# A two-layer hybrid transformer trunk: layer 1's filter spectra, and each norm's sums and first tile, are placed elsewhere

## The chip, the cores and the metric

The kernel runs on one core of one Trainium2 chip. The metric is device time in microseconds (us) of one execution. The core's engines run side by side, each through its own list of instructions in order: TensorE (PE, matrix products; its weight loads stand apart as PEld), VectorE (DVE), ScalarE (ACT), GpSimd (POOL) and SyncE (SP, which issues the transfers). Instructions of different engines wait for one another by semaphores.

## The reference

A trunk of two layers (width 1024) works on 256 latent tokens and 256 context tokens; in the second layer the context only gives keys and values. Cut to what matters here:

```python
for l in range(DEPTH):
    mod = (act_lat @ w_mod[l] + b_mod[l])            # shift, scale and gate for each norm
    sh1, s1, g1, sh2, s2, g2 = split(mod, 6)
    p = modulate(x, norm1_w, sh1, s1) @ w_in         # rms_norm(x, w) * (1 + s) + sh
    x = x + g1 * parallel_mixers(p, attn, lp)        # attention, hyena, pool, gmlp; @ w_out
    h = modulate(x, norm2_w, sh2, s2)
    x = x + g2 * ((silu(h @ wg) * (h @ wu)) @ wd)
return rms_norm(x, final_norm_w)

def hyena_filters(n, lp):                            # inside the hyena mixer
    hdn = ...                                        # small sine network of the positions
    filt = (hdn @ hy_w3) * exp(-t * abs(hy_decay))
    k = concat(fwd, 0, reversed bwd)
    return k / sum(abs(k), axis=0)
kf = rfft(hyena_filters(n, lp), n=2 * n)             # the filter spectra
```

In layer 0 the same is done for the context tokens, so its matrix products carry 512 tokens, those of layer 1 (behind the keys and values) 256. All is float32.

## The kernel before

Activations lie transposed: eight tiles `x[j]` of 128 channels by 512 tokens. A large product is made of three fp32r matmuls (`mm3`, lines 209 to 211): each operand is split into a high part (`whi`, `hh`, a cast on ScalarE, L171 for weights) and a rest (`wlo`, `hl`, a subtraction on VectorE, L174 for weights), and high by high, low by high and high by low are added up in PSUM. Weights come as units of 512 KB in the order of `unit_order`; each of them is one transfer (`load_next`), one cast, one subtraction and 24 matmuls of 128x128 by 512 columns in layer 0. Between the units of layer 0 stand tiles `w_t`, mixed in evenly: a `w_t` tile is a piece of a modulation matrix, and VectorE makes 128 modulation values from it by two reductions (`mod_tile`, L259). Layer 0's FFN has 66 units, in two halves of 22 `w_ff` and 11 `w_dn` units, and 40 such tiles (`TILES1`) are mixed in between the third unit and the last two.

Modulation values that are not made so come in chunks (`CHUNKS`): eight transfers of 256 KB, each with four small matmuls on TensorE (`psmod`, L289) and a transposition on VectorE behind them. `chunk_load` issues the transfers, `chunk_mods` the matmuls. Chunk 4 is loaded in layer 0's product with `w_out`, chunk 5 (layer 1, tiles 16 to 19) in the second half of layer 0's FFN, chunk 6 in layer 1's `w_out`; `LOADAT` holds at which of the eight output tiles.

**A norm.** The last product of a stage ends with `residual` (L1186) for the eighth tile. The squares of the first seven tiles have been added into `acc` on VectorE by then (`sumsq_add`), the eighth's are made by ScalarE (`last_sq`, L326). `rstd` adds both over the channels with one-column matmuls (`pmss`, L336), four pairs for 512 tokens and two pairs for 256; VectorE scales the sums (L340), GpSimd takes the power -1/2 (L342), VectorE writes it on a diagonal (`dg`, L350), and TensorE spreads it over the partitions (`psrb`, L357, a float32 matmul). `norm_tiles` then makes the eight tiles of the product's input: VectorE multiplies with `psrb` (`nt`, L372), ScalarE scales and shifts each half of the tokens (`nh`, L375) and casts (`hh`, L376), VectorE subtracts (`hl`, L381). The products behind it begin with tile 0: `k_major` (tile `pmk`) with the first three `w_ff` units in norm 2, `wide_gen` (tile `pmw`, L621) in norm 1 of layer 1. The last norm has the sums and GpSimd's step alone; its transposed tiles (`psfin`) are scaled and stored.

**The spectra of layer 1** are made in the second half of layer 0's FFN by `spectra_gen(1)`, a generator that goes one step behind each output tile: transfers of `w3` and `dec`, four float32 matmuls with the network's output (`pspf`, L454), the window and the sums of absolute values, a reciprocal (L475), splits, and five spectra (A0, A1, B0, B1, C0) of six fp32r matmuls each (`pssp`) against constants.

The program is written unit by unit; a scheduler orders each engine's instructions from it, so those of neighbouring steps lie between one another.

## Time and profile before

| what | value |
|---|---|
| median of 3 runs | 1348.98 us (1348.16 to 1349.43) |
| the profiled execution | 1349.05 us |
| its span | 1347.3 us |
| PE busy | 1304.3 us (97%) |
| VectorE busy | 925.6 us (69%) |
| ScalarE busy | 607.1 us (45%) |
| GpSimd busy | 64.2 us (5%) |
| mean granted TensorE clock | 0.981 |

The span is what the profile's times count from; 1.75 us of the execution lie outside of it. A busy PE is one in which a matmul is in flight. The granted clock is 1.00 where TensorE ran at 2.4 GHz and 0.50 where it ran at 1.2 GHz; a stretch between holds some of both.

### The profile page before, as it was taken

Reading aid. Unit: us, or ns where it says so; the run is one execution under the profiler, and the core shown is the slowest. Engines: PE = TensorE matmul, PEld = TensorE weight load, DVE = VectorE, ACT = ScalarE, POOL = GpSimd, SP = SyncE. Lnnn points to the kernel's source line nnn. Section 1 sums busy time; section 2 is a strip of 40 time slices with the busy share of each in tenths; the row PEclk is TensorE's granted clock in tenths of the full one; section 3 lists DMA queues with packets and bytes.
Section 4 is the critical chain, followed back from the end, with each engine's and each line's share of the span. In section 5 each row is a group of like instructions: output and inputs, shape, how many; then the busy total and the mean of one; then the engine's idle time right before and its main releaser. Section 6 shows DMA issues by size and latency. Waiting matters only on the chain.

```text
span 1347.3 us, 20114 instructions
## 1 busy us (share of the span) xinstructions
PE 1304.3 (97%) x7778; PEld 1135.4 (84%) x7778; DVE 925.6 (69%) x1578; ACT 607.1 (45%) x1059; POOL 64.2 (5%) x69
## 2 busy tenths in 40 slices
PE   4999999999999999999999999989999999999997
PEld 4778788888888877888888887879989998999997
DVE  3688778798977456666566666856789866655554
ACT  3563323467753326222222224255458854543443
POOL 0001400300000000000000000001310000000000
PEclk7999999999999999999999999989999999999999
DMA  9541334343345452555455553433334467465561
GB/s 345 199 140 62 102 111 145 114 141 106 121 142 166 162 188 68 166 162 167 144 175 167 160 165 124 160 126 124 127 116 144 138 194 254 143 187 179 182 187 49
DMA packets 68640, 203.86 MB, mean 151 GB/s; under 512 B 7616, under 2 KB 13888, under 8 KB 68544
## 3 DMA queue, kind: packets, MB, share of 16 engines
q1 hardware_dynamic: 68544, 202.58, 46.7%
q8 instruction: 61, 1.00, 0.3%
q14 instruction: 35, 0.29, 0.1%
HBM read 201.50 MB, written 1.05 MB: 150 GB/s over the span
## 4 chain that ended last, share of the span: by engine, by line
PE 72%; issue 16%; DVE 6%; ACT 2%; POOL 1%; DMA 1%; SPq 0%; DVEq 0%; POOLq 0%; ACTq 0%
PE pmn L209 14%; PE pmn L211 14%; PE pmn L210 14%; PE pmd L210 3%; PE pmd L211 3%; PE pmd L209 3%; PE pmb L209 2%; PE pmb L211 2%; PE pmb L210 2%; DVE wlo L174 2%; PE pmw L621 2%; PE psav L1132 1%; PE pmw L623 1%; PE pmw L622 1%; PE pspt L1110 1%
## 5 line engine op out<-in xcount | busy, mean ns | idle before, releaser
L171 ACT CAST whi<-raw 128x1024 fp32r<-128x1024 f32 (+2 forms) x312 | 288.1, 929 | 493.3 <-PE pmn L210 208.4
L209 PE MATMUL pmn<-hh,whi 128*128 128x512 f32 (+1 forms) x1328 | 450.8, 339 | 0.3 <-DVE vst L665 0.3
L211 PE MATMUL pmn<-hh,wlo 128*128 128x512 f32 (+1 forms) x1328 | 448.8, 338 | 0.3 <-DVE wlo L174 0.3
L210 PE MATMUL pmn<-hl,whi 128*128 128x512 f32 (+1 forms) x1328 | 449.0, 338 | 0.0
L174 DVE TENSOR_TENSOR wlo<-raw,whi 128x1024 fp32r<-128x1024 f32 (+2 forms) x312 | 335.9, 1079 | 164.4 <-ACT whi L171 161.4
L209 PEld LDWEIGHTS pmn<-hh,whi 128*128 128x128 f32 x1328 | 252.8, 190 | 27.3 <-DVE vst L665 0.7
L211 PEld LDWEIGHTS pmn<-hh,wlo 128*128 128x128 f32 x1328 | 252.5, 190 | 27.5 <-issue 1.1
L210 PEld LDWEIGHTS pmn<-hl,whi 128*128 128x128 f32 x1328 | 252.6, 190 | 26.2 <-issue 0.5
L259 DVE CUSTOM_DVE_ANT_0 junk<-raw,cb,pack_a 128x1024 bf16<-128x1024 f32 x136 | 176.8, 1300 | 1.5
L209 PE MATMUL pmd<-hh,whi 128*128 128x512 f32 (+1 forms) x352 | 120.2, 341 | 0.0
L210 PE MATMUL pmd<-hl,whi 128*128 128x512 f32 (+1 forms) x352 | 119.3, 339 | 0.0
L211 PE MATMUL pmd<-hh,wlo 128*128 128x512 f32 (+1 forms) x352 | 118.5, 337 | 0.0
L210 PEld LDWEIGHTS pmd<-hl,whi 128*128 128x128 f32 x352 | 66.9, 190 | 7.9 <-issue 1.2
L209 PEld LDWEIGHTS pmd<-hh,whi 128*128 128x128 f32 x352 | 66.9, 190 | 7.4 <-issue 0.7
L211 PEld LDWEIGHTS pmd<-hh,wlo 128*128 128x128 f32 x352 | 66.9, 190 | 7.3 <-issue 0.5
L1242 DVE TENSOR_TENSOR sg<-sg,pmn 128x512 f32<-128x512 f32 (+1 forms) x42 | 23.3, 554 | 67.5 <-PE pmn L211 67.5
L342 POOL TENSOR_TENSOR rs<-rs,halfexp 128x4 f32<-128x4 f32 (+1 forms) x5 | 5.4, 1078 | 971.6 <-DVE rs L340 971.6
L621 PE MATMUL pmw<-whi,hh 128*128 128x512 f32 (+1 forms) x112 | 45.1, 403 | 6.8 <-ACT hh L376 6.8
L375 ACT ACTIVATE nh<-nt,mod,amod 128x256 f32<-128x256 f32 x56 | 30.7, 593 | 42.4 <-DVE nt L372 37.1
L622 PE MATMUL pmw<-wlo,hh 128*128 128x512 f32 (+1 forms) x112 | 43.5, 388 | 0.0
L623 PE MATMUL pmw<-whi,hl 128*128 128x512 f32 (+1 forms) x112 | 43.2, 389 | 0.0
L1186 DVE SCALAR_TENSOR_TENSOR x<-pmd,mod,x 128x256 f32<-128x256 f32 x48 | 21.8, 477 | 24.8 <-PE pmd L211 24.8
(270 smaller groups left out, 1888.6 us busy)
## 6 DMA issues: line engine op xcount, KB each, us to landing
raw<-in_w_ff SPq DMA_DIRECT2D x88, 512.0 KB, 3.7
raw<-in_w_nar SPq DMA_DIRECT2D x84, 512.0 KB, 3.7
raw<-in_w_t SPq DMA_DIRECT2D x68, 512.0 KB, 3.7
raw<-in_w_dn SPq DMA_DIRECT2D x44, 512.0 KB, 4.1
raw<-in_w_mod SPq DMA_DIRECT2D x56, 256.0 KB, 5.7
raw<-in_w_wide SPq DMA_DIRECT2D x16, 512.0 KB, 3.7
raw<-in_w_out SPq DMA_DIRECT2D x16, 512.0 KB, 4.3
raw<-in_w_br SPq DMA_DIRECT2D x48, 128.0 KB, 2.1
```

The source lines that it names most:

```text
L171: S.copy(hi[:, :n], raw[:, :n])
L174: V.tensor_sub(lo[:, :n], raw[:, :n], f32(hi[:, :n]))
L209: T.matmul(o, lhsT=wh, rhs=xh, start=first, stop=False)
L210: T.matmul(o, lhsT=wh, rhs=xl, start=False, stop=False)
L211: T.matmul(o, lhsT=wl, rhs=xh, start=False, stop=last)
L259: r = V.tensor_tensor_reduce(out=junk, in0=raw, in1=cb[:, s, :], scale=1.0, scalar=bmod[:, l, i : i + 1], op0=ALU.mult, op1=ALU.add, accum ...
L375: S.activation(h[:, a0:a1], t[:, a0:a1], AF.Identity, bias=sh, scale=a[:, j, k : k + 1])
L621: T.matmul(os_[t][:, :n], lhsT=hh[:, sl], rhs=wh, start=(kt == 0), stop=False)
L622: T.matmul(os_[t][:, :n], lhsT=hh[:, sl], rhs=wl, start=False, stop=False)
L623: T.matmul(os_[t][:, :n], lhsT=hl[:, sl], rhs=wh, start=False, stop=(kt == 7))
L1186: V.scalar_tensor_tensor(x[j][:, sl], o[:, sl], mod[l][:, gi * 8 + j, k : k + 1], x[j][:, sl], op0=ALU.mult, op1=ALU.add)
L1242: V.tensor_mul(sg[:, CS], sg[:, CS], o[:, CS])
```

## The change

1. **Tiles in place of a chunk.** Chunk (1, 4) is dropped; its tiles (1, 16) to (1, 19) become `w_t` tiles, 44 in place of 40 in layer 0's FFN, mixed in between its sixth unit and its last four.
2. **Sums in two calls.** `rstd` is split: `sums_of` for `acc` is issued ahead of the last residual, and one for the last squares behind it.
3. **First tile.** For norms without a `between` argument (norm 2 of both layers, norm 1 of layer 1) `norm_tiles` makes tile 0 by two `scalar_tensor_tensor` on VectorE (x times scale times `psrb`, one for each 256 tokens), from which ScalarE writes `hh` and VectorE `nh`.
4. **Filters.** The transfers of `w3` and `dec` for layer 1 go to layer 0's `w_out`, ahead of chunk 4's. The four `pspf` matmuls are written at layer 0's second norm, and their results are copied to SBUF by ScalarE (`filter_keep`).
5. **Spectra.** `spectra_gen(1)` ends with the split parts, which get the tiles `hh4` to `hh7` and `hl4` to `hl7`. The matmuls of the five spectra are written from the last residual of layer 0's FFN on, around `rstd` and `rstd_bcast`; VectorE's part of A0, A1 and C0 (`spectrum_out`) goes between the norm's tiles 2 to 4.
6. The transfer of `skip` is issued behind those of the transform's constants.

```diff
-LOADAT = (4, 6)
+LOADAT = 4
-TILES1 = [(1, i) for i in (*range(16), *range(20, 24), *range(24, 40), *range(44, 48))]
+TILES1 = [(1, i) for i in (*range(40), *range(44, 48))]
-CHUNKS += [(l, tuple(range(4 * c, 4 * c + 4))) for l, c in ((0, 10), (1, 4), (1, 10))]
+CHUNKS += [(l, tuple(range(4 * c, 4 * c + 4))) for l, c in ((0, 10), (1, 10))]
...
-            ff = ff[:3] + mix(ff[3:-2], TILES1) + ff[-2:]
+            ff = ff[:6] + mix(ff[6:-4], TILES1) + ff[-4:]
...
+    def sums_of(o, v, c0, c1, first, last):
         nt = (c1 - c0) // P
-        o = bank("ss")
         for t in range(nt):
             sl = slice(c0 + t * P, c0 + t * P + P)
-            for i, v in enumerate(sums):
-                T.matmul(
-                    o[:, t : t + 1], lhsT=v[:, sl], rhs=ones[:, 0:1], start=(i == 0), stop=(i == len(sums) - 1)
-                )
+            T.matmul(
+                o[:, t : t + 1], lhsT=v[:, sl], rhs=ones[:, 0:1],
+                start=first and t == 0, stop=last and t == nt - 1,
+            )
...
+                short = between is None and j == js[0]
+                if not short:
+                    V.tensor_mul(t[:, sl], x[j][:, sl], rb[:, sl])
                 for a0, a1, k in spans:
                     sh = mod[l][:, 24 * which + j, k : k + 1]
-                    S.activation(h[:, a0:a1], t[:, a0:a1], AF.Identity, bias=sh, scale=a[:, j, k : k + 1])
-                S.copy(hi[:, sl], h[:, sl])
+                    if short:
+                        V.scalar_tensor_tensor(
+                            t[:, a0:a1], x[j][:, a0:a1], a[:, j, k : k + 1], rb[:, a0:a1], op0=ALU.mult, op1=ALU.mult
+                        )
+                        S.activation(hi[:, a0:a1], t[:, a0:a1], AF.Identity, bias=sh)
+                        V.tensor_scalar(h[:, a0:a1], t[:, a0:a1], sh, None, op0=ALU.add)
...
+    def filter_mm(l, p, o):
+        w3, _, f = flt[l]
+        f[p, o] = side("pf")
+        T.matmul(f[p, o], lhsT=hk[:, p * P : p * P + P], rhs=w3[o], start=True, stop=True)
+
+    def filter_keep(l, p, o):
+        f = flt[l][2]
+        t = t2(s="fo")
+        S.copy(t, f[p, o])
+        f[p, o] = t
...
+            if j == KT - 1:
+                so = bank("ss")
+                sums_of(so, acc, C0, NTOK, True, False)
+                if full:
+                    filter_mm(1, 0, 0)
             residual(o, j, 2)
...
-            if j == LOADAT[0]:
-                chunk_load(4 if full else 6)
-        last = last_sq(x, C0, NTOK)
-        r2 = rstd([acc, last], C0, NTOK)
+            if j == LOADAT:
+                if full:
+                    filters_load(1)
+                chunk_load(4 if full else 5)
+        sums_of(so, last_sq(x, C0, NTOK), C0, NTOK, False, True)
+        r2 = rstd(so, C0, NTOK)
+        if full:
+            filter_mm(1, 0, 1)
         chunk_mods(BUB[0])
         rb = rstd_bcast(r2, C0, NTOK)
+        if full:
+            filter_mm(1, 1, 0)
         chunk_mods(BUB[1])
...
+        if full:
+            for po in ((0, 0), (0, 1), (1, 0)):
+                filter_keep(1, *po)
+            filter_mm(1, 1, 1)
+            filter_keep(1, 1, 1)
...
-        last = last_sq(x, C0, NTOK)
-        r2 = rstd([acc, last], C0, NTOK)
+        sums_of(so, last_sq(x, C0, NTOK), C0, NTOK, False, True)
+        r2 = rstd(so, C0, NTOK)
         if full:
-            chunk_mods(BUB[0])
+            spectrum_out(1, "B0", skip)
+            spectrum_mm(1, "B1", parts, fwd, nyq)
+            spectrum_out(1, "B1", skip)
+            spectrum_mm(1, "A0", parts, fwd, nyq)
             rb = rstd_bcast(r2, C0, NTOK)
-            chunk_mods(BUB[1])
+            spectrum_mm(1, "A1", parts, fwd, nyq)
+            spectrum_mm(1, "C0", parts, fwd, nyq)
```

What the scheduler makes of it is seen in the lists of instructions. First TensorE's at layer 0's second norm, from the small matmuls of the chunk (`psmod`) to the matmul that spreads the norm's factor (`psrb`); in the list before one sum of `acc` and five transfers' `psmod` stand ahead of these rows.

```order
L289 MATMUL psmod_4684<-raw_4558,csf 32x128 x4
L289 MATMUL psmod_4684<-raw_4560,csf 32x128
L336 MATMUL pmss_4671<-ones,sq_4669 128x1
L336 MATMUL pmss_4671<-ones,acc_4369 128x1
L336 MATMUL pmss_4671<-ones,sq_4669 128x1
L336 MATMUL pmss_4671<-ones,acc_4369 128x1
L336 MATMUL pmss_4671<-ones,sq_4669 128x1
L336 MATMUL pmss_4671<-ones,acc_4369 128x1
L336 MATMUL pmss_4671<-ones,sq_4669 128x1
L289 MATMUL psmod_4684<-raw_4560,csf 32x128 x3
L289 MATMUL psmod_4684<-raw_4562,csf 32x128 x4
L357 MATMUL psrb_4703<-dg_4701,ones 128x512
```

The same place now, from the last matmul of `w_out` (`pmn`) on.

```order
L211 MATMUL pmn_4644<-mgh_4349,wlo_4598 128x512
L334 MATMUL pmss_4675<-ones,acc_4369 128x1 x4
L463 MATMUL pspf_4680<-w_1060_4548,hyh 128x512
L463 MATMUL pspf_4694<-w_1061_4549,hyh 128x512
L334 MATMUL pmss_4675<-ones,sq_4684 128x1 x4
L289 MATMUL psmod_4696<-raw_4556,csf 32x128 x4
L289 MATMUL psmod_4696<-raw_4558,csf 32x128 x4
L289 MATMUL psmod_4696<-raw_4560,csf 32x128 x4
L289 MATMUL psmod_4696<-raw_4562,csf 32x128 x4
L289 MATMUL psmod_4696<-raw_4564,csf 32x128
L360 MATMUL psrb_4715<-dg_4713,ones 128x512
L289 MATMUL psmod_4696<-raw_4564,csf 32x128 x3
```

Four sums stand ahead of the residual's wait and four behind it; between them stand two filter matmuls (`pspf`; the `w` that they read is `w3`). Behind `psrb` come the rest of the chunk's fifth transfer and its last three, 15 small matmuls. Of the other two filter matmuls one lies among `k_major`'s rows and one behind them.

Second, TensorE's list at layer 1's first norm, before, with the end of dropped chunk (1, 4).

```order
L289 MATMUL psmod_7371<-raw_7300,csf 32x128 x4
L289 MATMUL psmod_7371<-raw_7302,csf 32x128 x4
L336 MATMUL pmss_7358<-ones,sq_7356 128x1
L336 MATMUL pmss_7358<-ones,acc_4887 128x1
L336 MATMUL pmss_7358<-ones,sq_7356 128x1
L336 MATMUL pmss_7358<-ones,acc_4887 128x1
L336 MATMUL pmss_7358<-ones,sq_7356 128x1
L336 MATMUL pmss_7358<-ones,acc_4887 128x1
L336 MATMUL pmss_7358<-ones,sq_7356 128x1
L289 MATMUL psmod_7371<-raw_7304,csf 32x128 x4
L289 MATMUL psmod_7371<-raw_7306,csf 32x128 x4
L357 MATMUL psrb_7390<-dg_7388,ones 128x512
```

The same place now; `pssp_7341` is B1, `pssp_7350` A0 and `pssp_7361` A1.

```order
L210 MATMUL pssp_7341<-fl_7164,dft_fh_869 128x512
L211 MATMUL pssp_7341<-fh_7163,dft_fl_870 128x512
L209 MATMUL pssp_7350<-fh_7099,dft_fh_863 128x512
L334 MATMUL pmss_7315<-ones,sq_7329 128x1 x4
L210 MATMUL pssp_7350<-fl_7100,dft_fh_863 128x512
L211 MATMUL pssp_7350<-fh_7099,dft_fl_864 128x512
L209 MATMUL pssp_7350<-fh_7104,dft_fh_869 128x512
L210 MATMUL pssp_7350<-fl_7105,dft_fh_869 128x512
L211 MATMUL pssp_7350<-fh_7104,dft_fl_870 128x512
L360 MATMUL psrb_7359<-dg_7357,ones 128x512
L209 MATMUL pssp_7361<-fh_7099,dft_fh_863 128x512
L210 MATMUL pssp_7361<-fl_7100,dft_fh_863 128x512
```

Eight spectrum matmuls lie between the two groups of sums (the last three are seen here), five ahead of `psrb`, and twelve (A1 and C0) between `psrb` and the first `pmw`; four of B0's and one of B1's stay among the `pmd` matmuls of the FFN's second half.

Third, ScalarE's list at the same norm, before, from the last squares to the second tile's cast.

```order
L326 ACTIVATE sq_7356<-x_4367 128x512
L375 ACTIVATE nh_7397<-nt_7396,mod_89,amod_92 128x256 x2
L375 ACTIVATE nh_7405<-nt_7404,mod_89,amod_92 128x256
L376 CAST hh_7398<-nh_7397 128x512
L375 ACTIVATE nh_7405<-nt_7404,mod_89,amod_92 128x256
L375 ACTIVATE nh_7434<-nt_7433,mod_89,amod_92 128x256
L376 CAST hh_7406<-nh_7405 128x512
```

The same now.

```order
L326 ACTIVATE sq_7329<-x_4367 128x512
L556 COPY spec_7339<-pssp_7320 128x512
L556 COPY spec_7348<-pssp_7341 128x512
L384 ACTIVATE hh_7377<-nt_7375,mod_89 128x256 x2
L387 ACTIVATE nh_7386<-nt_7385,mod_89,amod_92 128x256 x2
L389 CAST hh_7387<-nh_7386 128x512
```

Two copies of spectra (B0, B1) stand ahead of the first tile, whose cast and whose interleaved scaling of tile 1 are gone.

## Rows read from the trace of the kernel before

**Rows 1.** The page's first part: engine, busy us (share of span), instructions.
```profile
PE 1304.3 (97%) x7778; PEld 1135.4 (84%) x7778; DVE 925.6 (69%) x1578; ACT 607.1 (45%) x1059; POOL 64.2 (5%) x69
```

**Rows 2.** Windows: busy us (instructions) of PE, PEld, DVE, ACT, POOL, clock, DMA, GB/s.
```profile
502.00:508.00 6.00, 2.62 (x3) 1.00 (x4) 2.87 (x5) 2.69 (x6) 0.00 (x0) 0.50 0.23 82
...
888.00:896.00 8.00, 5.04 (x12) 3.14 (x13) 4.76 (x9) 5.24 (x11) 0.00 (x0) 0.50 0.00 0
...
1146.00:1150.00 4.00, 4.00 (x23) 4.00 (x22) 3.43 (x12) 3.94 (x11) 0.00 (x0) 0.58 0.02 7
```

**Rows 3.** Timeline, layer 0's second norm: start, us, engine, instruction, [idle before <-releaser].
```profile
496.07 1.72 PE L289 MATMUL psmod<-raw,csf 128*32 128x128 f32 x50
...
497.71 0.38 PE L336 MATMUL pmss<-ones,sq 128*128 128x1 f32 x2
...
499.48 0.16 DVE L340 TENSOR_SCALAR rs<-pmss 128x4 f32<-128x4 f32 x1
499.56 1.28 DVE L259 CUSTOM_DVE_ANT_0 junk<-raw,cb,pack_a 128x1024 bf16<-128x1024 f32 x1
499.72 1.98 POOL L342 TENSOR_TENSOR rs<-rs,halfexp 128x4 f32<-128x4 f32 x1 [232.71 <-DVE rs L340]
...
502.48 2.08 PE L357 MATMUL psrb<-dg,ones 128*128 128x512 f32 x2 [2.47 <-DVE dg L350]
...
507.45 1.65 PE L209 MATMUL pmk<-hh,whi 128*128 128x512 f32 x3 [2.90 <-ACT hh L376]
...
511.83 0.40 PE L209 MATMUL pmk<-hh,whi 128*128 128x512 f32 x1
```

**Rows 4.** The page's groups: one half tile on ScalarE, one on VectorE.
```profile
L375 ACT ACTIVATE nh<-nt,mod,amod 128x256 f32<-128x256 f32 x56 | 30.7, 593 | 42.4 <-DVE nt L372 37.1
...
L1186 DVE SCALAR_TENSOR_TENSOR x<-pmd,mod,x 128x256 f32<-128x256 f32 x48 | 21.8, 477 | 24.8 <-PE pmd L211 24.8
```

**Rows 5.** Timeline of PE alone, second half of layer 0's FFN.
```profile
821.07 1.13 PE L454 MATMUL pspf<-w,hyh 128*128 128x512 f32 x2 [0.31 <-DMA w<-in_hy_w]
...
823.25 1.13 PE L454 MATMUL pspf<-w,hyh 128*128 128x512 f32 x2 [0.37 <-DMA w<-in_hy_w]
...
826.76 1.88 PE L454 MATMUL pspf<-w,hyh 128*128 128x512 f32 x4
828.07 0.79 PE L209 MATMUL pmd<-hh,whi 128*128 128x512 f32 x1
828.70 0.40 PE L210 MATMUL pmd<-hl,whi 128*128 128x512 f32 x1
```

**Rows 6.** Windows of layer 0's FFN, columns as in group 2.
```profile
514.00:690.00 176.00, 176.00 (x778) 145.85 (x777) 111.64 (x155) 50.69 (x63) 0.00 (x0) 1.00 0.49 153
...
830.00:850.00 20.00, 20.00 (x86) 15.76 (x85) 18.56 (x31) 6.80 (x10) 0.00 (x0) 1.00 0.31 102
850.00:866.00 16.00, 16.00 (x71) 12.98 (x71) 15.02 (x22) 5.35 (x7) 0.00 (x0) 1.00 0.57 174
```

**Rows 7.** Timeline, layer 1's first norm.
```profile
886.08 1.01 POOL L342 TENSOR_TENSOR rs<-rs,halfexp 128x4 f32<-128x4 f32 x1 [384.39 <-DVE rs L340]
...
887.87 2.08 PE L357 MATMUL psrb<-dg,ones 128*128 128x512 f32 x2 [1.49 <-DVE dg L350]
...
892.91 0.58 PE L621 MATMUL pmw<-whi,hh 128*128 128x256 f32 x1 [2.96 <-ACT hh L376]
...
897.87 0.40 PE L621 MATMUL pmw<-whi,hh 128*128 128x512 f32 x1
```

**Rows 8.** Timeline, layer 1's second norm: the first tile.
```profile
1143.43 1.08 DVE L372 TENSOR_TENSOR nt<-x,psrb 128x256 f32<-128x256 f32 x3 [0.85 <-PE psrb L357]
...
1145.32 0.62 PE L209 MATMUL pmk<-hh,whi 128*128 128x256 f32 x3 [1.93 <-ACT hh L376]
```

**Rows 9.** Timeline, the last norm: three sums, then their scaling.
```profile
1339.45 0.38 PE L336 MATMUL pmss<-ones,sq 128*128 128x1 f32 x2 [0.69 <-ACT sq L326]
...
1340.31 0.16 DVE L340 TENSOR_SCALAR rs<-pmss 128x2 f32<-128x2 f32 x1 [1.37 <-PE pmss L336]
```

More of the change, by code (lines that the diff above doesn't have):

```diff
@@ L436, in trunk_kernel, with filters_load @@
     spectra = {}
-    def spectra_gen(l):
-        if l == 0:
-            yield from mlp_gen()
+    flt = {}
+    def filters_load(l):
         w3 = [t2(s="w3") for _ in range(2)]
@@ L446, in spectra_gen @@
             SY.dma_start(out=dec[o], in_=I["hy_decay"][l, o * 512 : o * 512 + 512].partition_broadcast(P))
+        flt[l] = w3, dec, {}
+    def filter_mm(l, p, o):
[7 more added lines that the diff above has]
+        f[p, o] = t
+    def spectra_gen(l):
+        if l == 0:
+            yield from mlp_gen()
+            filters_load(l)
+        _, dec, fs = flt[l]
+        for o in range(2):
             S.activation(dec[o], dec[o], AF.Abs)
@@ L449, in spectra_gen @@
         for p in range(2):
-            f = [t2(s="fo") for _ in range(2)]
+            f = []
             s_, d_ = t2(s="fs"), t2(s="fd")
             for o in range(2):
-                pf = side("pf")
-                T.matmul(pf, lhsT=hk[:, p * P : p * P + P], rhs=w3[o], start=True, stop=True)
+                if l == 0:
+                    filter_mm(l, p, o)
+                    f.append(t2(s="fo"))
+                else:
+                    f.append(fs[p, o])
                 win = t2(s="win")
                 S.activation(win, dec[o], AF.Exp, scale=hy_negt[:, p : p + 1])
-                V.tensor_mul(f[o], pf, win)
+                V.tensor_mul(f[o], fs[p, o], win)
                 if p == 0:
@@ new lines, in spectra_gen @@
+                if l == 0:
+                    hi, lo = t2(F32R, "fh"), t2(F32R, "fl")
+                else:
+                    n = 4 + 2 * k + p
+                    hi = xp.tile([P, NTOK], F32R, tag=f"hh{n}", name=nm("fh"))
+                    lo = xp.tile([P, NTOK], F32R, tag=f"hl{n}", name=nm("fl"))
+                split(hi, lo, sd[p][k])
+                ps_.append((hi, lo))
+            parts.append(ps_)
+            if l == 0:
+                if k == 0:
+                    yield
+                for name in (("A0", "A1"), ("B0", "B1", "C0"))[k]:
+                    spectrum_mm(l, name, parts, fwd, nyq)
+                    spectrum_out(l, name, skip)
+            else:
+                yield
@@ new lines, in spectra_gen, with spectrum_mm, spectrum_out @@
+        flt[l] = parts, fwd, nyq, skip
+    def spectrum_mm(l, name, parts, fwd, nyq):
+        k, col, mat = {
+            "A0": (0, 0, fwd), "A1": (0, 128, fwd), "B0": (1, 0, nyq), "B1": (1, 384, fwd), "C0": (0, 128, nyq)
+        }[name]
+        o = side("sp")
+        for p in range(2):
+            h, lo = mat[p]
+            mm3(o, h[:, col : col + P], lo[:, col : col + P], *parts[k][p], p == 0, p == 1)
+        spectra.setdefault(l, {})[name] = o
+    def spectrum_out(l, name, skip):
+        t = t2(s="spec")
+        o = spectra[l][name]
+        if name in ("A0", "A1", "C0"):
+            V.tensor_add(t, o, skip)
+        else:
+            S.copy(t, o)
+        spectra[l][name] = t
@@ L649, in trunk_kernel @@
         else:
-            for h in norm_tiles(l, 0, x, rb, 0, NTOK, range(KT)):
+            for i, h in enumerate(norm_tiles(l, 0, x, rb, 0, NTOK, range(KT))):
                 hs.append(h)
                 os_ = next(w0)
-                chunk_mods(REST)
+                if i in (2, 3, 4):
+                    spectrum_out(1, ("A0", "A1", "C0")[i - 2], flt[1][3])
         sg_ = spectra_gen(0) if l == 0 else iter(())
@@ L1260, in trunk_kernel @@
                         done()
+                if half == 1 and j == KT - 1:
+                    for _ in sg_:
+                        pass
+                    so = bank("ss")
+                    sums_of(so, acc, C0, NTOK, True, False)
+                    if full:
+                        parts, fwd, nyq, skip = flt[1]
+                        spectrum_mm(1, "B0", parts, fwd, nyq)
                 residual(o, j, 5)
@@ L1269, in trunk_kernel @@
                 next(sg_, None)
-                if full and half == 1 and j == LOADAT[1]:
-                    chunk_load(5)
-            for _ in sg_:
-                pass
-        last = last_sq(x, C0, NTOK)
-        r2 = rstd([acc, last], C0, NTOK)
+        sums_of(so, last_sq(x, C0, NTOK), C0, NTOK, False, True)
+        r2 = rstd(so, C0, NTOK)
         if full:
-            chunk_mods(BUB[0])
+            spectrum_out(1, "B0", skip)
+            spectrum_mm(1, "B1", parts, fwd, nyq)
+            spectrum_out(1, "B1", skip)
+            spectrum_mm(1, "A0", parts, fwd, nyq)
             rb = rstd_bcast(r2, C0, NTOK)
-            chunk_mods(BUB[1])
+            spectrum_mm(1, "A1", parts, fwd, nyq)
+            spectrum_mm(1, "C0", parts, fwd, nyq)
     final_weigh(KT - 1)
```

38 lines of the change are left out of this document (13 added, 25 removed).

## The prediction, on record before the changed kernel ran

> **What bounds the kernel now.** The page's busy times come first: TensorE is busy for 1304.3 us of the span of 1347.3, VectorE for 925.6, ScalarE for 607.1 [rows 1]. So time can be won in two ways: work taken off TensorE where it is dense, and shorter waits in the few gaps. The windows by stage come next. In layer 0's FFN TensorE is busy without a break (176.00 of 176.00 us, 20.00 of 20.00, 16.00 of 16.00 [rows 6]); what leaves it there shortens the span one for one. In the second of these, VectorE is busy for 18.56 of 20 us, so a second engine is near its limit. The gaps are the norms. There the clock is the second price: 0.50 from 502 to 508 and from 888 to 896, 0.58 from 1146 to 1150 [rows 2]; 0.50 is 1.2 GHz, so matmuls behind the gap take twice as long. The timeline shows the chain of a gap: last sums, VectorE's scaling, GpSimd's power, `psrb`, the first tile, the first `pmk` or `pmw` [rows 3, 7].
>
> **Terms from rows.** A 512-column fp32r matmul at full clock takes 16.00 / 71 = 0.225 us [rows 6]. Two filter matmuls and one `pmd` lie between 826.76 and 828.70: (1.94 - 0.225) / 2 = 0.86 us for one filter matmul [rows 5]. `psrb` has the same shape and type: 2.08 us as the gaps show it [rows 3, 7], about 1.0 at full clock (0.86 and the pipeline's end). Seven sums end just before 499.48: (499.43 - 497.71) / 7 = 0.25 each [rows 3]. A `psmod` record takes 1.72 / 50 = 0.034 [rows 3].
>
> **Dense part of layer 0's FFN.** 25 of 30 spectrum matmuls leave it: 25 x 0.225 = 5.6 us. Two of the four filter matmuls go into the norm's gap: 2 x 0.86 = 1.7; the other two stay in dense stretches, at the norm's product. The waits for `w3` (0.31 and 0.37) go [rows 5], since the transfers are now issued some three output units, about 16 us, ahead of use: 0.7. Together **8.0 us**. VectorE gets eight more L259 of 1.28 us, 10.2 us, less a little work on the dropped chunk; ScalarE four copies of half a microsecond. I cost them at nothing: TensorE covers them, as VectorE has 64 us free of 176 in the longest stretch [rows 6]. Without this cover they cost what the third and fourth cases say. The dropped chunk's 2 MB are replaced by four tiles of 512 KB, so transfers stay equal.
>
> **Gap at layer 0's second norm.** The last residual's product ends near 495.9. Four sums (1.0), two filter matmuls (1.7) and four sums (1.0) in one queue end at about 499.5: the scaling at 499.48 stays where it is. The earlier sums gain nothing here, because the filters take their place. GpSimd's power took 1.98 us with an L259 of a tile alongside it on VectorE [rows 3] and 1.01 in the other gap, where none ran [rows 7]; the tile leaves this gap: gain 0.97 (bounds 0 and 0.97; I take the near row, since it is the same operation). From `psrb`'s end (502.48 + 2.08 = 504.56) to the first `pmk` at 507.45 it was 2.89 us [rows 3]. Now one half tile on VectorE, 0.48, then two on ScalarE, 2 x 0.59 [rows 4], with hand-offs 1.73: gain 1.16. The rest is the clock. Before, TensorE idled for 2.47 and then 2.90 us, and its clock came back only at 511.83; the ten matmuls between 507.45 and there took 4.38 us, where 2.25 would do: a loss of 2.1 [rows 3]. Now `psrb` is wanted at 501.5, after an idle of 0.9, and 30 `psmod` records (1.0) fill the wait for the first tile. If the clock stays up, `psrb` gives 1.1 and the matmuls 2.1 more: 0.97 + 1.16 + 1.1 + 2.1 = 5.3. If it falls, the leftover `psmod` take 2.0 at half speed and hold the first `pmk` until 502.48 - 0.97 + 2.08 + 2.0 = 505.6: a gain of 1.85. No row decides between these; I take the middle, **3.6**.
>
> **Gap at layer 1's first norm.** Eight spectrum matmuls (1.8) and the first four sums (1.0) hold the last four sums until about 886.05, some 0.2 later than the 885.84 that GpSimd's start at 886.08 implies [rows 7]. `psrb` comes at 888.1. TensorE is idle for only some 0.9 us ahead of it instead of 1.49, and the twelve matmuls of A1 and C0 stand behind it, so I take the clock to stay up: `psrb` ends at 889.1, A1 and C0 at 889.1 + 12 x 0.225 = 891.8. The first tile is ready at 889.1 + 1.73 = 890.8, hidden. Before, `pmw` began at 892.91 at half clock and had done 12 matmuls of 256 and 6 of 512 columns by 897.87 [rows 7]; at full clock these are worth 12 x 0.225 = 2.7, a start at 895.2. Gain 895.2 - 891.8 = **3.4**. If the clock falls all the same, `psrb` ends at 890.2 and the twelve take 4.96 us, as those of before did: 895.1, a gain of 0 if the clock is back by then and a loss of 2.2 if the next products are slow too. Bounds -2.2 and 3.4. The two copies on ScalarE run while it waits.
>
> **The clock rule.** The Trainium skill (TensorE: Matmul & The Clock Gate, HAM oscillation) says that a TensorE that waits between groups of matmuls drops to half rate, and that each next group then starts slow. Both gaps keep waits after the change, so by this rule alone the second case below holds, at 1338.0; the rows agree as to both gaps before.
>
> **The other norms.** Layer 1's second norm: first tile from 1143.43 to 1145.32, 1.89 us [rows 8]; now 0.48 + 0.59 and hand-offs, 1.2: gain 0.7. One sum fewer stands behind the last squares, here and in the last norm, where three sums and the hand-off took 0.86 us [rows 9]: about 0.22 each. Together **1.1** (bounds 0.4, if transfers hold the small matmuls there, and 2.8, if the slow stretch from 1146 to 1150, worth (1 - 0.58) x 4 = 1.7, goes as well [rows 2]).
>
> **Sum.** 8.0 + 3.6 + 3.4 + 1.1 = 16.1. The profiled execution took 1349.05 us, 1.75 outside the span, and stands 0.07 above the median: 1349.05 - 16.1 = 1332.9.
>
> **The cases.**
> First, as summed: **1332.9**, its own range 1329.3 (5.3 and 2.8 instead of 3.6 and 1.1) to 1337. Chance 0.60.
> Second, the clock falls in both gaps all the same. For it: it fell in both before, and a queue of one-column sums stands in each. Against it: shorter idle times. 8.0 + 1.85 + 0 + 1.1 = 11.0: **1338.0**, down to a gain of 8.7, 1340.3, with the loss of 2.2. Chance 0.20.
> Third, VectorE becomes the bound where layer 1's filters are made. From 830 to 866 it is busy for 33.6 of 36 us [rows 6]; 44 tiles over 56 units in place of 40 over 61 add 0.13 tile, 0.35 us, to a unit of 24 x 0.225 = 5.4 us: 2.3 more, 35.9 of 36. It decides if the work comes in bunches; a late `wlo` then costs up to 3 us: **1336**. Chance 0.12.
> Fourth, on the slow side: TensorE waits for `wlo` throughout layer 0's FFN, because a tile's two reductions (2.6) stand ahead of it. A unit with a tile, a `wlo` and the gating's work fills nearly 5.4 us. The point is 16.1 / 56 = 0.29 us of waiting for each of the 56 units; at 0.4 it loses 22.4: **1355**. Against it: VectorE was busy for only 112 of 176 us, and units are split ahead of use [rows 6]. Chance 0.05, of which 0.02 within 0.2%.
> Fifth, the change does not do what it says: the filters wait for `w3` in the gap, with the sums queued behind. At 2 us each it costs 4: **1337**. Against it is the lead of 16 us. Chance 0.03.
>
> **How the numbers follow.** Two runs' medians can be told apart from 0.2%, 2.7 us. Faster: all cases but the fourth, 0.95; same 0.02; slower 0.03. The range takes the first case's low end and the second's high end: 1329 to 1341; the fourth and the far ends are left out.
>
> **What would show it.** Right: no `pspf` and about five `pssp` in the FFN's second half; GpSimd's power near 1.0 in layer 0's second norm; `psrb` near 1.0 and a clock near 1.00 behind layer 1's first norm, with `pmw` right behind the spectra; first tiles 0.7 to 1.2 us shorter. Wrong: windows with 0.50 behind `psrb`; PE waits for `wlo` in layer 0's FFN; waits for `w` ahead of the sums. The forecast falls if the dense part doesn't lose its 8 us.

## The result and the profile after

The changed kernel takes 1328.99 us (median of 4 runs, 1327.81 to 1329.54); the kernel before took 1349.2 beside it (1348.16 to 1349.55). The ratio is 0.9852, with an interval of 0.984 to 0.9864. Run again later beside other kernels, it took 1327.89 against 1346.67: 0.986 (0.9839 to 0.9881). By the medians the change is worth 20.2 us in the first comparison and 18.8 in the second. The forecast was 1332.9, from 1329 to 1341; the result lies on the low end of this range (0.01 us below it; the later median lies 1.1 below it, with the kernel before 2.5 faster as well).

The first part of the page of the changed kernel, to be read against [rows 1]:

```profile
PE 1292.9 (98%) x7714; PEld 1128.2 (85%) x7714; DVE 935.6 (71%) x1599; ACT 608.6 (46%) x1060; POOL 61.9 (5%) x69
```

TensorE is busy for 11.4 us less, while the span is shorter by 21.3 (1347.3 to 1326.0). Little computation has gone: filters and spectra are all still made, and only the dropped chunk's 64 `psmod` records, some 2.2 us at 0.034 each, are gone. The rest of the fall in busy time is matmuls that ran at half clock and now run at full clock; the remaining 9.9 us of the gain are idle time.

Windows of the changed kernel behind the three norms (columns as in [rows 2]), and one of the end of layer 0's FFN:

```profile
500.00:504.00 4.00, 3.49 (x40) 2.34 (x40) 3.69 (x8) 2.54 (x6) 0.00 (x0) 1.00 0.02 6
...
872.00:876.00 4.00, 4.00 (x18) 3.02 (x19) 2.92 (x7) 1.80 (x4) 0.00 (x0) 1.00 0.00 0
...
1126.00:1130.00 4.00, 4.00 (x25) 4.00 (x25) 3.38 (x11) 3.82 (x10) 0.00 (x0) 0.68 0.02 9
...
830.00:850.00 20.00, 20.00 (x87) 16.02 (x86) 20.00 (x33) 9.04 (x13) 0.00 (x0) 1.00 0.38 132
```

The clock is 1.00 where [rows 2] had 0.50 twice; in layer 1's second norm it is 0.68 here, and was 1.00 in the second profile of the same kernel. From 830 to 850 VectorE is busy for 20.00 of 20 us; the kernel before had 19.69 in its fullest such stretch (840 to 860), so this is not far from what it was.

Layer 0's second norm now (timeline; start, us, engine, instruction, idle before it), against [rows 3]:

```profile
494.33 1.96 PE L463 MATMUL pspf<-w,hyh 128*128 128x512 f32 x4
...
496.13 0.95 PE L334 MATMUL pmss<-ones,sq 128*128 128x1 f32 x8
...
497.12 0.16 DVE L343 TENSOR_SCALAR rs<-pmss 128x4 f32<-128x4 f32 x1 [1.27 <-PE pmss L334]
497.36 1.01 POOL L345 TENSOR_TENSOR rs<-rs,halfexp 128x4 f32<-128x4 f32 x1 [232.66 <-DVE rs L343]
...
499.15 1.13 PE L360 MATMUL psrb<-dg,ones 128*128 128x512 f32 x2 [0.86 <-DVE dg L353]
500.20 1.07 PE L289 MATMUL psmod<-raw,csf 128*32 128x128 f32 x30
...
501.78 0.96 PE L209 MATMUL pmk<-hh,whi 128*128 128x512 f32 x3 [0.51 <-ACT hh L384]
```

Idle times of 0.86 and 0.51 us stand where 2.47 and 2.90 stood. `psrb` takes 1.13 in place of 2.08, and the 30 leftover `psmod` records fill most of the wait for the first tile.

Layer 1's first norm, against [rows 7]:

```profile
870.12 1.01 POOL L345 TENSOR_TENSOR rs<-rs,halfexp 128x4 f32<-128x4 f32 x1 [371.75 <-DVE rs L343]
...
871.91 1.13 PE L360 MATMUL psrb<-dg,ones 128*128 128x512 f32 x2 [0.80 <-DVE dg L353]
...
875.40 0.39 PE L211 MATMUL pssp<-fh,dl 128*128 128x512 f32 x1
...
875.63 0.28 PE L676 MATMUL pmw<-whi,hh 128*128 128x256 f32 x1
```

`pmw` follows the last spectrum matmul without a wait.

**Stage by stage.** The last squares (L326, ScalarE) of layer 0's second norm and of layer 1's first one cut each profile into three stretches:

| profile | start to squares, layer 0 | to squares, layer 1 | to the end | span |
|---|---|---|---|---|
| before | 496.97 | 386.43 | 463.90 | 1347.3 |
| changed | 494.69 | 372.62 | 458.69 | 1326.0 |
| changed, second profile | 496.00 | 372.77 | 457.33 | 1326.1 |

Ahead of the first squares the two kernels issue nearly the same work, yet 2.28 us are won there. The windows of the wait in the inverse transform, of before and of after, show where most of it is:

```profile
160.00:170.00 10.00, 8.30 (x30) 6.23 (x29) 8.60 (x18) 3.17 (x6) 1.51 (x2) 0.85 0.32 110
```

```profile
160.00:170.00 10.00, 8.30 (x36) 6.33 (x35) 7.98 (x16) 3.70 (x7) 0.84 (x2) 1.00 0.28 88
```

The first product behind the wait, of before and of after:

```profile
166.14 0.49 PE L209 MATMUL psiv<-yh,dft_ih 128*128 128x512 f32 x1 [1.47 <-ACT yh L142]
```

```profile
165.38 0.49 PE L209 MATMUL psiv<-yh,dft_ih 128*128 128x512 f32 x1 [1.47 <-ACT yh L142]
```

TensorE is busy for 8.30 us in both, with a wait of 1.47 us in both, and the clock fell behind it in one only. From these rows to the squares it is 330.83 us before and 329.31 after: 1.5 of the 2.28. Over ten profiles, of the changed kernel and of those below whose TensorE does the same up to there, the first stretch is 494.69 to 497.92 us; the kernel before's 496.97 lies inside. So this part of the difference is chance: it comes and goes from run to run.

### The profile page after: what moved, and what is told of

The parts are those of the page before. It is cut to its first block, busy times and chain, and to the rows that moved or that the text cites. A ratio compares the mean times of both kernels' runs of the same rounds, so it can differ in the third digit from the quotient of the medians.

```text
span 1326.0 us, 19996 instructions
## 1 busy us (share of the span) xinstructions
PE 1292.9 (98%) x7714; PEld 1128.2 (85%) x7714; DVE 935.6 (71%) x1599; ACT 608.6 (46%) x1060; POOL 61.9 (5%) x69
## 4 chain that ended last, share of the span: by engine, by line
PE 75%; issue 16%; DVE 5%; ACT 2%; POOL 1%; DMA 0%; DVEq 0%; POOLq 0%; ACTq 0%
PE pmn L209 14%; PE pmn L211 14%; PE pmn L210 14%; PE pmd L209 3%; PE pmd L210 3%; PE pmd L211 3%; PE pmb L209 2%; PE pmb L210 2%; PE pmb L211 2%; PE pmw L676 2%; PE pmw L678 2%; PE pmw L677 2%; PE psav L1188 1%; PE pspt L1166 1%; DVE wlo L174 1%
## 5 line engine op out<-in xcount | busy, mean ns | idle before, releaser
L259 DVE CUSTOM_DVE_ANT_0 junk<-raw,cb,pack_a 128x1024 bf16<-128x1024 f32 x144 | 187.0, 1299 | 1.4
L387 ACT ACTIVATE nh<-nt,mod,amod 128x256 f32<-128x256 f32 x51 | 28.0, 594 | 24.4 <-DVE nt L377 19.2
```

The source lines that it names most:

```text
L259: r = V.tensor_tensor_reduce(out=junk, in0=raw, in1=cb[:, s, :], scale=1.0, scalar=bmod[:, l, i : i + 1], op0=ALU.mult, op1=ALU.add, accum ...
L387: S.activation(h[:, a0:a1], t[:, a0:a1], AF.Identity, bias=sh, scale=a[:, j, k : k + 1])
```

## The experiments

Changes of stretches below are against the changed kernel's second profile; changes of medians against its 1327.89.

**The changed kernel again.**

> The changed kernel itself once more, beside the next three on one chip, so that they can be compared directly. Theory A (the part of its gain that lies ahead of the first edit, 2.3 us of clock in the first 494 us of the profile, is chance): ratio to the kernel before nearer to 0.9865 than to 0.985, and in another profile the stretch ahead of layer 0's second norm may be as long as before. Theory B (that part belongs to the change): ratio 0.985, the stretch 2 us shorter again.

Its first stretch was 496.00 us in place of 494.69, and in layer 1's second norm the clock stayed at 1.00. At 165 us it held as in the first profile; most of the 1.3 us lies ahead of that, in the first product of layer 0, where the clock was 0.90 from 30 to 60 in place of 0.95. The ratio of 0.986 is nearer to A, but the intervals of both runs hold both values; the ten first stretches decide for A.

**The clock by itself.** The kernel before, with matmuls that compute nothing needed:

```diff
+    def warmup(v, n, c0=0, c1=512):
+        for _ in range(n):
+            T.matmul(side("fill")[:, : c1 - c0], lhsT=ones, rhs=v[:, c0:c1], start=True, stop=True)
...
         chunk_mods(BUB[0])
+        if full:
+            warmup(acc, 2)
         rb = rstd_bcast(r2, C0, NTOK)
         chunk_mods(BUB[1])
+        if full:
+            warmup(acc, 2)
```

and in the same way one and two of them at layer 1's first norm.

> The kernel before with nothing but needless matmuls added (float32, 128x512, 0.86 us each at full clock, results unused): in layer 0's second norm one among the last sums, one ahead of psrb and two behind it, in layer 1's first norm one among the last sums and two behind psrb. It measures the clock by itself. Theory A (the clock falls there because TensorE waits, and that costs psrb 1.1 and the first products 2.1 to 2.2 in each of the two gaps): about 4 to 6.5 us faster than before, 1342.5 to 1345, clock near 1.00 behind both psrb, one added matmul ahead of the sums costing some tenths. Theory B (the clock falls because of the one-column sums, whatever is beside them): no gain, or up to 2 us slower: 1349 to 1351.

1342.57 us against 1346.34 beside it, ratio 0.9966 (0.9955 to 0.9977): 3.8 us faster by the medians, 4.6 by the ratio. Windows of the two gaps, against the first two of [rows 2]:

```profile
502.00:508.00 6.00, 4.11 (x11) 2.11 (x12) 3.82 (x6) 3.41 (x7) 0.00 (x0) 1.00 0.26 87
888.00:896.00 8.00, 7.04 (x42) 6.26 (x43) 6.47 (x12) 8.00 (x17) 0.00 (x0) 1.00 0.00 0
```

Work that only keeps TensorE busy brings the clock to 1.00 in both. In the profile the second stretch is 3.3 us shorter than before's and the third 3.2: together A's upper figure of 6.5. Of the third's 3.2 only 2.7 lie ahead of layer 1's second norm, and the rest, where nothing was added, is not the edit's. The runs as a whole give less, 3.8 to 4.6.

**Spectra back in the FFN.**

```diff
-            if l == 0:
+            if True:
...
-            spectrum_out(1, "B0", skip)
-            spectrum_mm(1, "B1", parts, fwd, nyq)
-            spectrum_out(1, "B1", skip)
-            spectrum_mm(1, "A0", parts, fwd, nyq)
             rb = rstd_bcast(r2, C0, NTOK)
-            spectrum_mm(1, "A1", parts, fwd, nyq)
-            spectrum_mm(1, "C0", parts, fwd, nyq)
```

> The changed kernel with one part undone: all 30 spectrum matmuls of layer 1 stand in the second half of layer 0's FFN again; the gap at layer 1's first norm is left to the norm alone (chunk (1, 4) stays dropped). Both theories: 25 x 0.225 = 5.6 us more in the dense part. Theory A (clock stays up without them): the first pmw starts 1.73 us behind the end of psrb in place of 2.7, and the sums lose 0.2 of delay: 5.6 - 1.2 = 4.4 slower than the changed kernel, 1333.4, ratio 0.988. Theory B (the spectra keep the clock up): psrb takes 2.08 in place of 1.1 and the first products lose 2.2 at half clock: 7.7 slower, 1336.7, ratio 0.991, with a clock of 0.50 behind psrb.

1335.09 us, 0.9914 (0.99 to 0.9929): 7.2 slower. The second stretch grew by 5.7, which is the dense part's 5.6. `psrb` and the window behind it:

```profile
880.07 2.08 PE L360 MATMUL psrb<-dg,ones 128*128 128x512 f32 x2 [2.07 <-DVE dg L353]
...
880.00:885.00 5.00, 3.82 (x8) 2.15 (x9) 2.83 (x8) 1.70 (x4) 0.00 (x0) 0.50 0.02 5
```

The idle time ahead of `psrb` is 2.07 again and the clock falls: theory B in kind, though its sum was 7.7. The third stretch grew by only 1.0, since the first product no longer waits for spectra.

**Filters back in the FFN**, with their transfers.

```diff
             yield from mlp_gen()
-            filters_load(l)
+        filters_load(l)
...
-                if l == 0:
-                    filter_mm(l, p, o)
-                    f.append(t2(s="fo"))
-                else:
-                    f.append(fs[p, o])
+                filter_mm(l, p, o)
+                f.append(t2(s="fo"))
...
-            for po in ((0, 0), (0, 1), (1, 0)):
-                filter_keep(1, *po)
-            filter_mm(1, 1, 1)
-            filter_keep(1, 1, 1)
```

> The changed kernel with one part undone: the four filter matmuls of layer 1 and the transfers of w3 and dec stand in the second half of layer 0's FFN again. Both theories: 1.7 us and the two waits for w3 (0.7) come back in the dense part; in layer 0's second norm the last sums can start when the squares are there, 0.8 earlier. Theory A (clock stays up without the filters in the gap): 1.6 slower than the changed kernel, 1330.6, ratio 0.9863. Theory B (the filters are part of what keeps the clock up there): psrb 1.1 and the first products 2.1 longer as well: 4.8 slower, 1333.8, ratio 0.9887.

1337.32 us, 0.993 (0.9915 to 0.9944): 9.4 slower, twice what B said. The waits of TensorE and `psrb` of layer 1's first norm:

```profile
PE pspf L463 <- DMA w<-in_hy_w: 1.1, 1, 1.1
...
878.88 2.07 PE L360 MATMUL psrb<-dg,ones 128*128 128x512 f32 x2 [2.07 <-DVE dg L353]
```

and the first product of layer 0's second norm:

```profile
502.17 1.35 PE L209 MATMUL pmk<-hh,whi 128*128 128x512 f32 x3 [1.51 <-ACT hh L384]
```

The second stretch is 7.1 longer and the third 2.0. Besides the filters (1.7), the wait for `w3` (1.1) and the clock in layer 0's norm (0.76 in the window from 500 to 505), the spectra follow the filters: with these late, only 16 spectrum matmuls are left for the gap in place of 25 (9 x 0.225 = 2.0 more in the FFN), none stands between the last sums and `psrb`, and the clock falls there too. In layer 0's norm the order changed as well: all 64 `psmod` records stand ahead of `psrb`, and without them behind it the wait for the first tile is 1.51 in place of 0.51. So this run undoes more than the part that its text named.

**The long first tile back.**

```diff
-                short = between is None and j == js[0]
+                short = False
```

> The changed kernel with one part undone: the first tile of each norm goes the long way again (multiply, scale, cast); all else as changed. Theory A (the terms of the prediction): the short way is worth 1.16 us in layer 0's second norm and 0.7 in layer 1's second norm, and nothing in layer 1's first norm, where the twelve spectrum matmuls of A1 and C0 hide it: 1.9 us slower than the changed kernel, 1330.9, ratio to the kernel before 0.9865. Theory B (the short way also is what keeps TensorE's clock up in layer 0's second norm): TensorE's wait there for the first tile grows from 0.51 to some 1.7 us, the clock falls, and 2.1 us more are lost: 1333.0, ratio 0.988, with windows of clock near 0.50 behind that wait.

1333.24 us, 0.9903 (0.9886 to 0.9919): 5.3 slower, more than either theory's sum. In layer 0's second norm:

```profile
503.75 1.32 PE L209 MATMUL pmk<-hh,whi 128*128 128x512 f32 x3 [1.90 <-ACT hh L389]
...
505.00:510.00 5.00, 5.00 (x17) 3.80 (x16) 4.41 (x10) 5.00 (x11) 0.00 (x0) 0.74 0.00 2
```

TensorE's wait for the tile is 1.90 in place of 0.51, and the clock falls behind it, as B says. The second stretch grew by 3.0 and the third by 1.2, together 4.2, near B's 4.0; the rest of the difference of medians is not explained by this one profile.

**A VectorE reduction beside GpSimd's power**, in layer 0's second norm, first bound to the scaled sums `r`, then to the sums `o` themselves. The first:

```diff
+        if beside:
+            V.tensor_tensor_reduce(
+                out=junk, in0=cb[:, 0, :], in1=cb[:, 1, :], scale=1.0, scalar=r[:, 0:1],
+                op0=ALU.mult, op1=ALU.add, accum_out=small([P, 1], F32, "ju"),
+            )
```

and in the second with `scalar=o[:, 0:1]`.

> The changed kernel with one needless 1024-wide reduction on VectorE (the shape of a modulation tile's, 1.28 us, result unused) that starts behind the scaling of the sums in layer 0's second norm, so that it runs beside GpSimd's power. Theory A (VectorE beside it is what made the power take 1.98 us): the power takes near 2.0 again in place of 1.01, and the norm ends 0.9 to 1.3 later: 1 us slower, 2 to 4 if TensorE's longer wait lets the clock fall. Theory B (the 1.98 came from something else, such as the transfers of that stretch): the power stays at 1.01, and only the reduction itself can hold up the diagonal, by 0.4.

> The changed kernel with the needless 1024-wide reduction of the run before it, but bound to the sums and not to their scaling, so that it starts some 0.1 us earlier, as the tile's reduction did in the kernel before (0.16 us ahead of GpSimd's power); all of the chunk's small matmuls now stand ahead of the spreading matmul. Theory A (a VectorE instruction that has begun holds GpSimd's power up): the power takes near 1.98 again, and the norm is 1 to 4 us slower with the clock falling. Theory B (the power's 1.98 had another cause): the power stays at 1.01 as in the run before, where the reduction began only 0.04 ahead of it.

Their timelines at that place, the first:

```profile
497.78 1.32 DVE L346 CUSTOM_DVE_ANT_0 junk<-cb,rs 128x1024 bf16<-128x1024 f32 x1
497.82 1.01 POOL L350 TENSOR_TENSOR rs<-rs,halfexp 128x4 f32<-128x4 f32 x1 [232.68 <-DVE rs L343]
```

and the second:

```profile
500.44 1.28 DVE L346 CUSTOM_DVE_ANT_0 junk<-cb,pmss 128x1024 bf16<-128x1024 f32 x1
500.60 1.98 POOL L350 TENSOR_TENSOR rs<-rs,halfexp 128x4 f32<-128x4 f32 x1 [232.69 <-DVE rs L343]
```

With a lead of 0.04 us the power takes 1.01, with a lead of 0.16 it takes 1.98 and ends 0.86 behind the reduction's end (500.44 + 1.28 = 501.72). So the 1.98 of [rows 3] goes with the tile's reduction, which has a lead of 0.16 there too; that a reduction runs beside the power is not enough. The Trainium skill (SBUF — State Buffer, Terms) says that VectorE and GpSimd share a pair of ports that one of them holds for a whole instruction; the second timeline agrees, with the 0.86 us behind the reduction's end. The first does not: the reduction began first by the trace and took 1.32, the power 1.01, and neither was held up for the other's length.

The two runs took 1330.88 (0.9885) and 1331.6 (0.9881), 3.0 and 3.7 slower, but this is not the price of the power. The first products of the norm, the first run and the second:

```profile
502.40 1.41 PE L209 MATMUL pmk<-hh,whi 128*128 128x512 f32 x3 [1.51 <-ACT hh L389]
```

```profile
506.00 1.65 PE L209 MATMUL pmk<-hh,whi 128*128 128x512 f32 x3 [1.51 <-ACT hh L389]
```

In both all 64 `psmod` records stand ahead of `psrb` and none behind it, so the wait for the first tile is 1.51 in place of 0.51, and the clock falls behind it, in the first run although the power took 1.01 and TensorE waited only 0.33 ahead of `psrb`. The second stretch is 1.6 and 2.3 longer.

**More work on VectorE.**

```diff
-        for s in range(2):
+        for s in (0, 1, 0) if l == 1 and n % 4 == 0 else (0, 1):
```

> The changed kernel with 11 needless reductions more on VectorE (every fourth modulation tile of layer 0's FFN makes one of its two twice): 11 x 1.28 = 14 us of VectorE work, more than the four tiles added (10.2). Theory A (VectorE has room, the tiles cost nothing): within 0.5 us of the changed kernel. Theory B (VectorE is at its limit where the filters are made; its busy share from 830 to 850 is 20.00 of 20 us in the changed kernel): TensorE waits for the subtracted part of a weight there, 1 to 4 us slower, with such waits in the list of TensorE's waits.

1329.45 us, 0.987 (0.9854 to 0.9887): 1.6 slower, within the intervals. The second stretch is 0.8 longer, and two waits that the changed kernel has not stand in the list of TensorE's waits:

```profile
PE pssp L209 <- ACT fh L142: 0.6, 1, 0.6
PE pstot L506 <- DVE fa L500: 0.4, 1, 0.4
```

14 us of VectorE work cost about 1 us, by the sums and splits of the filters and not by a weight: between the theories.

**The chunk back, with 40 tiles.**

```diff
-TILES1 = [(1, i) for i in (*range(40), *range(44, 48))]
+TILES1 = [(1, i) for i in (*range(16), *range(20, 24), *range(24, 40), *range(44, 48))]
...
-CHUNKS += [(l, tuple(range(4 * c, 4 * c + 4))) for l, c in ((0, 10), (1, 10))]
+CHUNKS += [(l, tuple(range(4 * c, 4 * c + 4))) for l, c in ((0, 10), (1, 4), (1, 10))]
...
-            ff = ff[:6] + mix(ff[6:-4], TILES1) + ff[-4:]
+            ff = ff[:3] + mix(ff[3:-2], TILES1) + ff[-2:]
```

> The changed kernel with one part undone: chunk (1, 4) is loaded and multiplied as before, 40 tiles in place of 44, mixed in from the third unit to the last two. Theory A (the part brings the tile out of layer 0's norm and 64 small matmuls out of layer 1's): 2.2 us of psmod come back in layer 1's first norm, where TensorE now has no idle time for them but some 0.8, and the power in layer 0's norm takes 1.98 again with a clock that may fall: 2.5 to 6 us slower than the changed kernel, 1330.5 to 1334. Theory B (the chunk's small matmuls fill waits, and VectorE's relief is worth something): within 1 us.

1335.33 us, 0.9909 (0.9893 to 0.9926): 7.4 slower. In layer 0's second norm:

```profile
499.02 1.28 DVE L259 CUSTOM_DVE_ANT_0 junk<-raw,cb,pack_a 128x1024 bf16<-128x1024 f32 x1
499.18 1.98 POOL L345 TENSOR_TENSOR rs<-rs,halfexp 128x4 f32<-128x4 f32 x1 [232.75 <-DVE rs L343]
...
504.58 1.65 PE L209 MATMUL pmk<-hh,whi 128*128 128x512 f32 x3 [1.51 <-ACT hh L384]
...
505.00:510.00 5.00, 5.00 (x13) 3.84 (x13) 4.28 (x9) 4.83 (x10) 0.00 (x0) 0.50 0.18 67
```

The tile's reduction, the power of 1.98 and the half clock are back, and so is the wait of 1.51, with all `psmod` ahead of `psrb`; the second stretch is 4.0 longer and the third, with the chunk's `psmod` among the spectra, 2.1. This is more than A's upper figure of 6.

**The sums behind the squares.**

```diff
+    def sums_both(o, v, w_, c0, c1):
+        for t in range((c1 - c0) // P):
+            sl = slice(c0 + t * P, c0 + t * P + P)
+            for i, u in enumerate((w_, v)):
+                T.matmul(o[:, t : t + 1], lhsT=u[:, sl], rhs=ones[:, 0:1], start=(i == 0), stop=(i == 1))
...
-        sums_of(so, last_sq(x, C0, NTOK), C0, NTOK, False, True)
+        so = bank("ss")
+        sums_both(so, acc, last_sq(x, C0, NTOK), C0, NTOK)
```

The calls of `sums_of` ahead of the residuals are gone with it.

> The changed kernel with one part undone: the sums of the first seven tiles' squares stand behind the last squares again, in all norms of this kind. Theory A (the queue of TensorE is what counts): in layer 0's norm 2 and layer 1's norm 1 filters and spectra then fill the time ahead of the squares, and the last sums end 0.1 to 1.0 later in each; in the two others one or two sums more are behind the squares, 0.2 to 0.4 each: 1 to 2.5 us slower, 1329 to 1330.5. Theory B (the split is worth nothing, since the filters and spectra take the time that it frees): within 0.5 us.

1332.64 us, 0.989 (0.9876 to 0.9903): 4.7 slower, more than A. The second stretch is only 0.2 longer: there the filters fill the time, as B says. The third is 4.4 longer: 1.7 of this lie between the squares of layer 1's two norms, and 2.8 behind those of the second, where the clock was 0.62 from 1126 to 1130. It was 0.68 in the changed kernel's first profile, whose time there is 1.4 longer than the second's, so half of the 2.8 may be chance. Layer 1's first norm:

```profile
874.24 2.01 PE L367 MATMUL psrb<-dg,ones 128*128 128x512 f32 x2 [0.80 <-DVE dg L360]
...
872.00:876.00 4.00, 3.20 (x10) 1.65 (x9) 0.86 (x2) 0.00 (x0) 1.01 (x1) 0.79 0.30 117
876.00:880.00 4.00, 4.00 (x17) 3.25 (x16) 3.71 (x8) 2.56 (x6) 0.00 (x0) 0.78 0.00 0
```

TensorE's idle time ahead of `psrb` is 0.80, the same as in the changed kernel, and the clock fell all the same. What differs ahead of it is that all eight sums stand together behind the squares. In the seven other profiles with 0.80 or 0.81 there the clock stayed up. One profile shows the fall; whether the sums are the cause, or chance as at 165 us, stays open.

**Filled versions of the changed kernel**: three needless matmuls near 27 us and two behind `psrb` of layer 1's second norm; in the second version one more in the wait near 165 us.

```diff
+                if g == 0:
+                    warmup(x[0], 3)
                 hs += norm_tiles(l, 0, x, rb, 0, NTOK, range(2 * g, 2 * g + 2), between)
...
+        if not full:
+            warmup(acc, 2, C0, NTOK)
...
+                            if l == 0 and tt == 0 and k == order[-1]:
+                                warmup(x[0], 1)
```

> The changed kernel with needless matmuls in two gaps that it leaves: three (float32, 128x512) ahead of the first product of layer 0 near 27 us, where TensorE then waits 3.3 us and goes on at half clock, and two (128x256) behind the matmul that spreads layer 1's second norm, where the clock was 0.68 from 1126 to 1130. Theory A (these waits let the clock fall): up to 1.7 us at the start and up to 1.6 in layer 1's norm: 2 to 3 us faster than the changed kernel, 1326 to 1327. Theory B (the clock there falls whatever TensorE does in the wait, or the added matmuls run slowly and hold up the products): no change, or 1 us slower.

> The changed kernel with the five needless matmuls of the filled version and one more (float32, 128x512) in the wait of 1.47 us near 165 us (the inverse transform's last part), behind which the clock is 0.83 to 0.87 in some profiles and 1.00 in others. Theory A (each of these waits lets the clock fall at some runs, and covering them ends it): 1 to 1.6 us ahead of the filled version at its median and 2 to 3 us ahead of the changed kernel, ratio 0.984, and less scatter between runs. Theory B (no gain from it): ratio 0.986.

The first took 1327.09 (0.9854; 0.9839 to 0.9869), 0.8 below the changed kernel, which cannot be told from none; theory A had 2 to 3. In its profile the clock held behind both filled waits, and fell to 0.83 behind the wait near 165 us. The second took **1325.74** (1325.42 to 1326.6; 0.9843, 0.983 to 0.9856), the fastest of all, some 2 us below the changed kernel and 1.4 below the first version, as A said, though the intervals of the ratios overlap. Windows of the second:

```profile
30.00:60.00 30.00, 28.91 (x283) 21.16 (x283) 16.52 (x32) 17.50 (x28) 2.08 (x8) 1.00 0.59 218
160.00:170.00 10.00, 9.11 (x38) 6.64 (x37) 7.85 (x17) 3.80 (x7) 0.81 (x1) 1.00 0.29 90
```

Its five runs spread over 1.2 us, the changed kernel's later four over 3.3 (1326.97 to 1330.3).

## Why the prediction was right, and where it was off

| term | predicted | profile |
|---|---|---|
| dense part of layer 0's FFN | 8.0 | 8.3 |
| layer 0's second norm | 3.6 (1.85 to 5.3) | 5.5 |
| layer 1's first norm | 3.4 (-2.2 to 3.4) | 3.5 |
| the other norms | 1.1 (0.4 to 2.8) | 1.7; 3.1 in the second profile |
| ahead of the first edit | 0 | 2.3 |

The profile's column is worked out as the prediction did it. The kernel before's first `pmk` at 507.45, with ten matmuls at half clock, is worth a start at 511.83 - 2.25 = 509.6. From the squares to there it is 12.6 us, and 494.69 to 501.78, 7.1, in the changed kernel: 5.5. What is left of the second stretch's 13.8 is 8.3. (Counted to the eleventh matmul instead, 511.83 and 504.45, it is 5.1 and 8.7: the border between the two terms is known to some 0.4.) In layer 1's first norm it is 883.40 to 895.2 against 867.31 to 875.63: 11.8 - 8.3 = 3.5, and the rest of the third stretch's 5.2 is 1.7. The five sum up to 21.3, the difference of the spans; the executions differ by 20.5, since 2.5 us of the changed one lie outside its span. Without the chance part the profiles' gain is 19.0 us, against a forecast of 16.1; most of the difference is layer 0's second norm. By the prediction's own terms the low end of its first case is 1329.55 (a gain of 8.0 + 5.3 + 3.4 + 2.8 = 19.5) and not 1329.3; the range's 1329 does not hang on it.

**Dense part: right.** Matmul count times 0.225 us, the filters' 0.86 and the vanished waits for `w3` gave the size. The run with the spectra put back shows 5.7 against 5.6. VectorE's tiles were rightly costed at next to nothing: TensorE has no wait of its own in the changed kernel from 514 to 866. But the cover is thin: 20.00 of 20 us, and 14 us more cost about 1.

**Layer 0's second norm: the mechanism was right, the size was not.** The prediction found 5.3 if the clock stays up and 1.85 if it falls, said that no row decides, and took the middle. It stayed up: 5.5. That is the term that was mis-sized, by 1.9. The middle of two outcomes is a value that neither of them gives. The second case, in which the clock falls in both gaps, did not occur. Nor does the rule in the prediction's paragraph on the clock, applied to any wait, hold here: waits of 0.86 and 0.51 in this norm and of 0.80 in layer 1's first one left the clock at 1.00.

The experiments say what the prediction found in no row. In the changed kernel and its variants, the wait for this norm's first tile was 0.51 in seven profiles, and the clock stayed up in all seven; it was 1.51 in four (filters back, chunk back, both reductions) and 1.90 in one (long tile), and the clock fell in all five. The wait is 0.51 where the short tile comes together with the 30 `psmod` records behind `psrb`; the prediction had both, and no row to weigh them by. The first of the reduction runs comes nearest to moving the 30 records alone: its power takes 1.01 and `psrb` starts only 0.15 later behind the squares, yet the wait is 1.51, the clock falls, and the second stretch is 1.6 longer. No run moves them with nothing else changed.

**GpSimd's power: right.** 1.01 us; the run with the reduction bound to the sums brings the 1.98 back, and the one before it shows that a reduction begun only 0.04 ahead does not.

**Layer 1's first norm: right.** The sums start the scaling later than before, `psrb` is at full clock, the spectra hide the first tile, and `pmw` follows them. Between the squares of layer 1's two norms both profiles of the changed kernel took 3.3 us less than the kernel before.

**The other norms: right in kind.** Short tile and fewer sums gave 1.7 us in one profile, where the clock fell behind the wait as before; in the other the clock held as well, and the 3.1 lie just above the upper bound of 2.8. In six of the eight profiles with the wait of 1.11 or 1.12 in layer 1's second norm and a full clock ahead of it, the clock held.

**What the prediction did not have** is the chance ahead of the first edit. It compared one profiled execution with a median, 0.07 apart, and took that for the whole of the scatter. The kernel before had its clock fall at 165 us in the profile, the changed one had not. Part of the 3.9 us by which the result stands below the forecast is therefore luck.

The rival of VectorE as the bound is seen only as a full window, without waits of TensorE. The slow rival and that of late transfers did not occur.

## What to carry to other kernels

Look for the clock behind each wait of the bounding engine, and give work that must be done anyway to the waits: the moved spectra paid twice, out of the dense part and by the clock that they kept. Look also at where the scheduler puts the small work: here 15 short matmuls (30 records) went with a full clock where they stood in a wait, and with half clock where they stood ahead of it. Where a term has two outcomes, forecast one of them and put the other into the range, rather than the middle. Undoing one part of such a change undoes the cover of its neighbours too, so five single parts undone cost 5 to 9 us each here, and their sum is more than the whole.
